# A decoder block's stick-breaking attention: scores by two products over all 128 rows, the weights' last product on GpSimd

## The chip, the cores and the metric

One core of one Trainium2 chip runs the whole kernel. The metric is the device time of one execution in microseconds (us).

## The reference

One decoder layer in float32: 1024 tokens of width 1024. It has eight heads of strictly causal stick-breaking attention and eight heads of latent attention (MLA) that share an input projection and an output projection, a gated feed-forward network with a short causal convolution, and a gated embedding at the end. What the change touches is the first of these:

```python
z = jnp.einsum('bqhd,bkhd->bhqk', q[:, start:end], k[:, :end]).astype(jnp.float32) * scale
strict = s_idx < t_idx
log_keep = jnp.where(strict, -jax.nn.softplus(z), 0.0)
log_keep_after = lax.cumsum(log_keep, axis=3, reverse=True) - log_keep
weights = jnp.where(strict, jnp.exp(jax.nn.log_sigmoid(z) + log_keep_after), 0.0)
outs.append(jnp.einsum('bhqk,bkhd->bqhd', weights.astype(v.dtype), v[:, :end]))
```

In words: the weight of key s for query t is sigmoid(z[t,s]) times the product of (1 - sigmoid(z[t,j])) over the keys j between s and t.

## The kernel before, in words

Every matrix product of the kernel is done in float32r with each operand split into a high part and a low part (`split`, lines 90 to 97: ScalarE copies the high part, VectorE or GpSimd subtracts it from the source to get the low one), and the small low-times-low term is dropped.

Stage 1 normalises and transposes the tokens. Stage 2, which the change touches, treats the eight stick-breaking heads as four pairs of two heads. A head has two units, g = 0 for the query blocks 0 to 3 (128 queries each) and g = 1 for the blocks 4 to 7. For block i, `sb_softmax` (lines 624 to 647) works on n = 128 (i + 1) keys, in one piece if n is at most 512 and otherwise in two halves (so a head has 12 pieces and 4608 columns of scores):

- TensorE forms the scores of a piece with two products: line 636, where the stationary operand holds the high part of the 64 query features beside the low part and the moving one holds the high part of the keys twice (128 rows), and line 637, high part of the queries times low part of the keys (64 rows); then the mask (line 447, through `masked`).
- ScalarE makes two sigmoids of it, of -z into `kc` (line 640) and of z into `w` (line 641).
- VectorE makes the running product of `kc` from the right with one scan (line 643), and multiplies `w` by it, shifted by one (line 645).

`kc` has two buffers that take turns. `weighted_sum` (lines 449 to 488) then transposes the blocks of `w` on TensorE (line 459), splits them (line 468) and multiplies by the values (lines 473, 474); line 479 adds the two halves into `o`, and line 674 stores a pair's `o` to the DRAM, a DMA in GpSimd's queue.

`run_units` (lines 490 to 510) writes the softmax of the next unit between the steps of the weighted sum of the unit before. Other work is spread between these steps by `Fill` (lines 151 to 191): during a pair, the projection of the next pair's queries, keys and values (`project`, lines 224 to 238; six times 24 products of 128 x 512), during the last pair `mla_prepare(True)`, the keys and values of the MLA heads with their stores in GpSimd's queue (lines 567, 575, 580). `mla_prepare(False)`, the MLA heads' queries, comes before the units in the program, and runs beside the first pair; GpSimd rotates its eight tiles of queries (`rotate`, lines 141 to 146) and stores them (line 610). A scheduler then fixes the order of instructions on each engine; an engine works its queue in this order. What it puts in front depends on a priority: the fill has 500 steps less than the rest (`LATER[0]`).

Of the kernel before, what the change touches and what calls it, by code (L numbers as in the profile page):

```python
# [21 lines left out]
NT = 8          # token tiles  # L22
NK = 8          # chunks of D_MODEL
H = 512         # tokens of a half
HD = 64
DFF = 2816
NCH = DFF // P  # 22
# [8 lines left out]
# how the work between the steps of the attention is spread: steps of it per step  # L36
# [5 lines left out]
# how far the scheduler is to put it behind the attention  # L42
LATER = (500, 0, 0, 2000)
# tiles normalised together in each half, and those scaled on the scalar engine
# [5 lines left out]
def tile_hybrid_block(ctx: ExitStack, tc: tile.TileContext, a: dict, out: bass.AP):  # L50
# [39 lines left out]
    def split(h, l, src, gain=None, on_pool=False):  # L90
        """src (times a gain of each partition) as the sum of two float32r parts."""
        if gain is None:
            act.copy(h, src)  # L93
            (pool if on_pool else dve).tensor_tensor(l, src, h, ALU.subtract)  # L94
        else:
            act.activation(h, src, AF.Copy, scale=gain)
            dve.scalar_tensor_tensor(l, src, gain, h, ALU.mult, ALU.subtract)
# [9 lines left out]
    def split_w(src, width=512, gain=None, on_pool=False, where=None):  # L107
        """A weight block of the DRAM, split."""
# [11 lines left out]
    def rstd_dve(small, ssq, count, n, tag, bufs=None):  # L120
        """(ssq / count + eps) ** -0.5 on one engine: Newton steps from a guess by exponent."""
# [16 lines left out]
    def rotate(eng, p_, x1, x2, cs, sn, shape):  # L138
        """The rotation of the pairs (x1, x2), in place."""
# [11 lines left out]
    class Fill:  # L151
        """Work traced in small steps between those of a stage. A generator gives True where it
        leaves none of the stage's buffers open."""
# [6 lines left out]
        def add(self, g, later=0):  # L160
            """later: how far behind the rest the scheduler is to put this work."""
            self.gens.append((g, later))
# [32 lines left out]
    now = {}                    # the current stage's makers of banks and of small tiles  # L195
# [17 lines left out]
    def sb_tiles(c):  # L213
        """Keys of two heads twice, their low parts, values; queries come later."""
        t4 = lambda tag: ata.tile([P, S], F32R, tag=tag, name=nm(tag), bufs=3)
        ka, kb = t4("ka"), t4("kb")
        kl = t4("ka" if c % 2 == 0 else "kb")
        vt = [ata.tile([P, NT, P], F32R, tag="v", name=nm("v"), bufs=3) for _ in range(2)]
        return {"k": (ka, kb), "kl": kl, "v": vt}
# [4 lines left out]
    def project(ci, consume, ths=(0, 1), ws=None):  # L224
        """128 columns of the input projection, transposed, for each half of the tokens."""
# [16 lines left out]
    def to_q(tiles):  # L242
        """Queries: the high part beside the low part."""
        def consume(th, ps):
            if th == 0:
                tiles["q"] = (tile4("qa", 2), tile4("qb", 2))
            sl = slice(th * H, th * H + H)
            for e in range(2):
                q = tiles["q"][e]
                split(q[hs[e], sl], q[hs[1 - e], sl], ps[hs[e], :])  # L250
        return consume

    def to_k(tiles):
        def consume(th, ps):
            sl = slice(th * H, th * H + H)
            for e in range(2):
                k = tiles["k"][e]
                split(k[hs[e], sl], tiles["kl"][hs[e], sl], ps[hs[e], :])
                act.copy(k[hs[1 - e], sl], k[hs[e], sl])
# [17 lines left out]
    with tc.tile_pool(name="pre", bufs=1) as pre, \  # L277
# [29 lines left out]
        # masks (rows are queries, columns keys)  # L307
# [7 lines left out]
        def normed(th):  # L315
            """A half of the tokens normalised, transposed and split."""
# [28 lines left out]
        # rotary tables  # L345
# [38 lines left out]
        def latents(th):  # L384
            """The latents of a half of the tokens, normalised, their keys' part rotated."""
# [14 lines left out]
            # the narrower part's sum doubled, so that one mean serves both  # L400
# [48 lines left out]
    def weighted_sum(u, p_, ptr, pav, rate):  # L449
        """The transposed product of a unit's weights with its values."""  # L450
# [30 lines left out]
        # the columns divided by their sums of weights: a row of each, the same in every partition  # L481
# [8 lines left out]
    def run_units(units, softmax, p_, ptr, pav, rates):  # L490
        """Softmax of each unit traced between the steps of the sum before it."""
# [52 lines left out]
    def mla_prepare(kv_only):  # L544
        """Latents to keys, values (kv_only) or queries of all MLA heads, kept in the DRAM."""
# [66 lines left out]

    for z in (project(0, to_q(pairs[0])), mla_prepare(False)):
# [10 lines left out]
    def sb_softmax(u):  # L624
        rows = hs[u["e"]]
        g, w = u["g"], u["w"]
        z = u["tiles"]
        q, k, kl = z["q"][u["e"]], z["k"][u["e"]], z["kl"]
        for i in range(4 * g, 4 * g + 4):
            n = (i + 1) * P  # L630
            qs = slice(i * P, i * P + P)
            kc = kcs[flip[0] % 2]
            flip[0] += 1
            for c0, c1 in pieces(n):
                sc = one_bank(py, "sc")[:, :c1 - c0]
                pe.matmul(sc, q[:, qs], k[:, c0:c1], start=True, stop=False)
                pe.matmul(sc, q[rows, qs], kl[rows, c0:c1], start=False, stop=c1 < n)
# [7 lines left out]
            dve.tensor_tensor(w[i], w[i], kc[:, S - n + 1:S + 1], ALU.mult)  # L645
# [5 lines left out]
    def sb_pre(u):  # L651
        c, g, e = u["c"], u["g"], u["e"]
        if e == 0 and g == 0:
            fill.drain()
            sb_pre.o = atb.tile([P, S], F32, tag="o", name=nm("o"), bufs=2)
            if c < 3:
                z = sb_tiles(c + 1)
                pairs.append(z)
                for ci, f_ in ((c + 1, to_q), (c + 5, to_k), (c + 9, to_v)):
# [25 lines left out]
    # --- MLA heads; between them the output projection of the stick-breaking heads, then of the  # L685
    # --- MLA heads' first half of the tokens, then the FFN of this half
# [11 lines left out]
    def group_ssq(src, sq, s, ps):  # L698
        """Sums of the squares over the features of (128, 4, 128) in token layout."""
# [642 lines left out]
```

## Time and profile before

| | |
|---|---|
| three runs | 1587.54, 1590.11 and 1591.46 us, median 1590.11 |
| the profiled execution | span 1588.5 us from the first to the last instruction |
| TensorE (PE) busy | 1507.7 us, 95% of the span |
| weight loads (PEld) busy | 1214.6 us, 76% |
| VectorE (DVE) busy | 1079.6 us, 68% |
| ScalarE (ACT) busy | 844.2 us, 53% |
| GpSimd (POOL) busy | 271.1 us, 17% |
| stick-breaking attention | from the first scores at 104.4 us to the first MLA scores at 417 us |

How to read it: "busy" is the time that an engine works on instructions; matmuls overlap, so their durations add up to more than the time in which they follow each other, and the spacing of their starts is the better measure. [...] Idle time is listed with what ended it: a tile of another engine, a DMA, or "issue", time in which an engine waited for nothing that the profile shows.

### The profile page before, as it was taken

The page shows a single profiled execution, that of the slowest core. Times are in us where ns is not written, and L with a number is a line of the kernel's source. Part 1 is how long each engine was busy: PE and PEld are TensorE (multiplying, and loading weights), DVE is VectorE, ACT ScalarE, POOL GpSimd, SP SyncE. Part 2 cuts the span into 40 slices and gives each one's busy share as a digit, 9 for nine tenths or more (in the row PEclk, how much of TensorE's full clock was granted, in tenths as well). Part 3 has the DMA queues.
Part 4 walks back from the last instruction along what each step waited for, and adds up shares of the span by engine and source line. Part 5 has one row for each costly group of instructions (what it writes and reads, how often), then busy time and mean ns, then how long its engine had stood idle before and what let it go on. Part 6 is the DMA issues. An engine that isn't in the chain of part 4 may idle for free. (4 is left out here: it accounts for less than half of the span.)

```text
span 1588.5 us, 20809 instructions
## 1 busy us (share of the span) xinstructions
PE 1507.7 (95%) x7032; PEld 1214.6 (76%) x7032; DVE 1079.6 (68%) x2021; ACT 844.2 (53%) x1649; POOL 271.1 (17%) x313
## 2 busy tenths in 40 slices
PE   4998999999899897999999999999999999999996
PEld 3976877766678786778888888888888888888875
DVE  4558667799767868866567954544986556544698
ACT  6345555677667756645544544444554444444542
POOL 7104300002133425242113100000000000000033
PEclk9998999999889999999999999999999999999998
DMA  6031210113345525134445532333443323333455
GB/s 197 22 100 40 86 48 27 41 52 126 111 134 148 157 70 186 61 99 146 148 125 169 177 119 90 97 95 96 141 134 94 98 94 94 93 93 94 132 176 169
DMA packets 109211, 173.78 MB, mean 109 GB/s; under 512 B 10912, under 2 KB 47680, under 8 KB 109104
## 3 DMA queue, kind: packets, MB, share of 16 engines
q1 hardware_dynamic: 100400, 142.71, 29.7%
q0 software_dynamic: 8704, 29.74, 5.0%
q8 instruction: 55, 0.90, 0.2%
q14 instruction: 52, 0.43, 0.1%
HBM read 142.26 MB, written 30.15 MB: 109 GB/s over the span
## 5 line engine op out<-in xcount | busy, mean ns | idle before, releaser
L93 ACT CAST wh<-ws 128x512 fp32r<-128x512 f32 x296 | 183.1, 620 | 213.3 <-PE mm L891 105.8
L94 DVE TENSOR_TENSOR wl<-ws,wh 128x512 fp32r<-128x512 f32 x281 | 199.9, 713 | 139.7 <-ACT wh L93 74.5
L889 PE MATMUL mm<-bh,wh 128*128 128x512 f32 x456 | 180.2, 395 | 0.0
L891 PE MATMUL mm<-bh,wh 128*128 128x512 f32 x456 | 180.1, 395 | 0.0
L94 DVE TENSOR_TENSOR fl<-f,fh 128x512 fp32r<-128x512 f32 x88 | 60.7, 691 | 118.0 <-PE mm L118 77.4
L94 DVE TENSOR_TENSOR tl<-tr,th 128x512 fp32r<-128x512 f32 x192 | 103.2, 549 | 33.9 <-ACT th L93 32.8
L895 PE MATMUL mm<-bh,wl 128*128 128x512 f32 x456 | 126.0, 396 | 0.0
L93 ACT CAST th<-tr 128x512 fp32r<-128x512 f32 x192 | 90.7, 483 | 64.6 <-PE tr L459 49.4
L643 DVE TENSOR_TENSOR_SCAN kc<-kc,one_f 128x128 f32<-128x128 f32 (+3 forms) x64 | 89.2, 1394 | 36.4 <-ACT kc L640 35.7
L93 ACT CAST fh<-f 128x512 fp32r<-128x512 f32 x88 | 54.6, 622 | 110.0 <-PE mm L117 84.3
L1160 POOL DMA_DIRECT2D x_dram<-fd x8 | 4.3, 538 | 615.1 <-DVE fd L1159 582.2
L459 PE MATMUL tr<-ident,w 128*128 128x128 f32 x576 | 103.3, 290 | 4.4 <-DVE tl L94 2.0
L889 PEld LDWEIGHTS mm<-bh,wh 128*128 128x128 f32 x456 | 85.9, 188 | 19.9
L891 PEld LDWEIGHTS mm<-bh,wh 128*128 128x128 f32 x456 | 85.9, 188 | 19.9
L895 PEld LDWEIGHTS mm<-bh,wl 128*128 128x128 f32 x456 | 85.6, 188 | 19.7
L116 PE MATMUL mm<-wh,fh 128*128 128x512 f32 x242 | 95.6, 396 | 0.0
L117 PE MATMUL mm<-wl,fh 128*128 128x512 f32 x242 | 95.3, 394 | 0.0
L459 PEld LDWEIGHTS tr<-ident,w 128*128 128x128 f32 x576 | 74.8, 148 | 20.0 <-DVE tl L94 3.7
L474 PE MATMUL av<-tl,v 128*128 128x512 f32 x192 | 75.8, 398 | 13.8 <-DVE tl L94 13.1
L473 PE MATMUL av<-th,v 128*128 128x512 f32 x192 | 79.2, 412 | 6.6 <-ACT th L93 3.6
L118 PE MATMUL mm<-wh,fl 128*128 128x512 f32 x242 | 82.5, 395 | 0.0
L640 ACT ACTIVATE kc<-sc 128x384 f32<-128x384 f32 (+4 forms) x96 | 47.7, 496 | 38.3 <-PE sc L447 22.9
(427 smaller groups left out, 3833.2 us busy)
## 6 DMA issues: line engine op xcount, KB each, us to landing
ws<-in_w_up SPq DMA_DIRECT2D x176, 256.0 KB, 2.6
ws<-in_w_down SPq DMA_DIRECT2D x88, 256.0 KB, 2.6
ws<-in_w_o SPq DMA_DIRECT2D x32, 256.0 KB, 2.8
xl<-x_dram SPq DMA_DIRECT2D x16, 512.0 KB, 3.9
ws<-in_w_in SPq DMA_DIRECT2D x24, 256.0 KB, 2.7
t<-o_dram SPq DMA_DIRECT2D x24, 256.0 KB, 3.2
xl<-o_dram SPq DMA_DIRECT2D x24, 256.0 KB, 2.8
xt<-in_x SPq DMA_DIRECT2D x8, 512.0 KB, 5.3
```

The lines of the kernel that those rows point to most:

```text
L93: act.copy(h, src)
L94: (pool if on_pool else dve).tensor_tensor(l, src, h, ALU.subtract)
L116: pe.matmul(ps, lh, rh, start=start, stop=False)
L117: pe.matmul(ps, lh, rl, start=False, stop=False)
L118: pe.matmul(ps, ll, rh, start=False, stop=stop)
L459: pe.transpose(tr[:, c:c + P], w[i][:, j * P:(j + 1) * P], ident)
L473: pe.matmul(av[:, lo:], v(j), th[:, lo:], start=j == 0, stop=False)
L474: pe.matmul(av[:, lo:], v(j), tl[:, lo:], start=False, stop=j == last)
L643: dve.tensor_tensor_scan(rev, rev, one_f[:, 0:1].to_broadcast([P, n]), 1.0, ALU.mult, ALU.mult)
L889: pe.matmul(ps, wh[:, k * P:(k + 1) * P], nh[:, kk], start=kk == 0, stop=False)
L891: pe.matmul(ps, wh[:, k * P:(k + 1) * P], nl[:, kk], start=False, stop=False)
L895: pe.matmul(ps, wl[:, k * P:(k + 1) * P], nh[:, kk], start=False, stop=kk == NK - 1)
```

## The change

Five edits, all in the stick-breaking part.

1. The keys lie as high part beside low part in one tile of 128 rows for each head (`to_k`), so their copy is gone. The queries lie twice (`to_q`): low part beside a copy of the high part (`q`), and high part beside zeros (`qz`, one of three tiles of 512 columns for each head of a pair, whose zero rows are written once). So line 642 of the new kernel multiplies `qz` by the keys (high times high, and zeros times low), and line 643 multiplies `q` by them (low times high and high times low): two products over 128 rows.
2. The product of `w` with the running product moves from VectorE (line 645) to GpSimd (line 651).
3. The projections of the next pair come in the order keys, values, queries instead of queries, keys, values.
4. `o` has one buffer instead of two.
5. The key tiles have two buffers instead of three.

```diff
     def sb_tiles(c):
...
-        t4 = lambda tag: ata.tile([P, S], F32R, tag=tag, name=nm(tag), bufs=3)
-        ka, kb = t4("ka"), t4("kb")
-        kl = t4("ka" if c % 2 == 0 else "kb")
+        ks = [ata.tile([P, S], F32R, tag=tag, name=nm(tag), bufs=2) for tag in ("ka", "kb")]
         vt = [ata.tile([P, NT, P], F32R, tag="v", name=nm("v"), bufs=3) for _ in range(2)]
-        return {"k": (ka, kb), "kl": kl, "v": vt}
+        return {"c": c, "k": ks, "v": vt}
...
             if th == 0:
                 tiles["q"] = (tile4("qa", 2), tile4("qb", 2))
+                tiles["qz"] = [[high_q[e][(2 * tiles["c"] + g) % 3] for g in range(2)]
+                               for e in range(2)]
             sl = slice(th * H, th * H + H)
             for e in range(2):
-                q = tiles["q"][e]
-                split(q[hs[e], sl], q[hs[1 - e], sl], ps[hs[e], :])
+                q, z = tiles["q"][e], tiles["qz"][e][th]
+                split(z[hs[e], :], q[hs[e], sl], ps[hs[e], :])
+                act.copy(q[hs[1 - e], sl], ps[hs[e], :])
...
                 k = tiles["k"][e]
-                split(k[hs[e], sl], tiles["kl"][hs[e], sl], ps[hs[e], :])
-                act.copy(k[hs[1 - e], sl], k[hs[e], sl])
+                split(k[hs[e], sl], k[hs[1 - e], sl], ps[hs[e], :])
...
+    high_q = [[atb.tile([P, H], F32R, name=f"qz{e}{i}") for i in range(3)] for e in range(2)]
+    for e in range(2):
+        for z in high_q[e]:
+            pool.memset(z[hs[1 - e], :].bitcast(F32), 0.0)
...
-                pe.matmul(sc, q[:, qs], k[:, c0:c1], start=True, stop=False)
-                pe.matmul(sc, q[rows, qs], kl[rows, c0:c1], start=False, stop=c1 < n)
+                pe.matmul(sc, qz[:, zs], k[:, c0:c1], start=True, stop=False)
+                pe.matmul(sc, q[:, qs], k[:, c0:c1], start=False, stop=c1 < n)
...
-            dve.tensor_tensor(w[i], w[i], kc[:, S - n + 1:S + 1], ALU.mult)
+            pool.tensor_tensor(w[i], w[i], kc[:, S - n + 1:S + 1], ALU.mult)
...
-            sb_pre.o = atb.tile([P, S], F32, tag="o", name=nm("o"), bufs=2)
+            sb_pre.o = atb.tile([P, S], F32, tag="o", name=nm("o"), bufs=1)
...
-                for ci, f_ in ((c + 1, to_q), (c + 5, to_k), (c + 9, to_v)):
+                for ci, f_ in ((c + 5, to_k), (c + 9, to_v), (c + 1, to_q)):
```

The scheduler makes a new order from this. Three places of it follow.

GpSimd's queue during the second head of the first pair. `w5` to `w7` are that head's weights, `qt` and `rt` belong to the rotation of the MLA queries, `q_dram` to their store. Before, the rotations of tiles stand there by themselves:

```order
L142 TENSOR_TENSOR rt_167_1092<-qt_163_1074,sin_t_85 128x128
L610 DMA q_dram_67<-qt_158_1048 128x4x192
L141 TENSOR_TENSOR rt_166_1091<-qt_163_1074,sin_t_85 128x128
L144 TENSOR_TENSOR qt_163_1074<-qt_163_1074,cos_t_84 128x8x16
L143 TENSOR_TENSOR qt_163_1074<-qt_163_1074,cos_t_84 128x8x16
L146 TENSOR_TENSOR qt_163_1074<-qt_163_1074,rt_166_1091 128x8x16
```

Now the products stand between them:

```order
L142 TENSOR_TENSOR rt_171_1129<-qt_167_1111,sin_t_85 128x128
L143 TENSOR_TENSOR qt_167_1111<-qt_167_1111,cos_t_84 128x8x16
L651 TENSOR_TENSOR w6_292_1688<-w6_292_1688,kc0_1267 128x896
L144 TENSOR_TENSOR qt_167_1111<-qt_167_1111,cos_t_84 128x8x16
L145 TENSOR_TENSOR qt_167_1111<-qt_167_1111,rt_171_1129 128x8x16
L651 TENSOR_TENSOR w7_293_1689<-w7_293_1689,kc1_1269 128x1024
L146 TENSOR_TENSOR qt_167_1111<-qt_167_1111,rt_170_1128 128x8x16
```

Of the 56 instructions of the eight rotations and their stores, 17 now stand between the first and the last product of this head, 2 ahead of them and 37 behind.

GpSimd's queue in the first head of the last pair. `k_dram`, `v_dram`, `kr_dram` and `o_dram` are stores, `kt` the first keys of the MLA heads. Before, there are only these:

```order
L989 TENSOR_TENSOR kt_835_3911<-ld_840_3916,kt_834_3910 96x512
L575 DMA k_dram_68<-lt_693_3379 128x512
L989 TENSOR_TENSOR kt_837_3913<-ld_841_3919,kt_836_3912 96x512
L580 DMA v_dram_70<-lt_695_3386 128x512
L567 DMA kr_dram_69<-lt_701_3412 32x512
L575 DMA k_dram_68<-lt_703_3419 128x512
```

Now the products of that head wait their turn between them:

```order
L995 TENSOR_TENSOR kt_831_3919<-ld_836_3924,kt_830_3918 96x512
L651 TENSOR_TENSOR w5_715_3484<-w5_715_3484,kc1_1269 128x768
L995 TENSOR_TENSOR kt_833_3921<-ld_837_3927,kt_832_3920 96x512
L577 DMA k_dram_68<-lt_689_3387 128x512
L582 DMA v_dram_70<-lt_691_3394 128x512
L680 DMA o_dram_63<-o_481_2536 128x1024
L569 DMA kr_dram_69<-lt_697_3420 32x512
L651 TENSOR_TENSOR w6_716_3485<-w6_716_3485,kc0_1267 128x896
L577 DMA k_dram_68<-lt_699_3427 128x512
L651 TENSOR_TENSOR w7_717_3486<-w7_717_3486,kc1_1269 128x1024
```

TensorE where the second pair begins. `pj` are projections, `sc` scores. Before, the pair's first scores stand behind 90 of the projections' products for that pair and are followed by the rest of them:

```order
L637 MATMUL sc_365_1971<-kb_201_1263,qa_231_1366 128x256
L447 MATMUL sc_365_1971<-mask_sb_78,ident_r_76 128x128
L116 MATMUL pj_278_1595<-hTh_2_96,wh_264_1510 128x512
L117 MATMUL pj_278_1595<-hTl_4_98,wh_264_1510 128x512
L118 MATMUL pj_278_1595<-hTh_2_96,wl_265_1511 128x512
```

Now all but four of the 144 (queries last) come first, and what follows the scores are the projections of the third pair (`pj_349`):

```order
L118 MATMUL pj_322_1813<-hTh_2_96,wh_306_1721 128x512
L643 MATMUL sc_353_1933<-ka_198_1272,qa_318_1790 128x128
L449 MATMUL sc_353_1933<-mask_sb_78,ident_r_76 128x128
L643 MATMUL sc_360_1978<-ka_198_1272,qa_318_1790 128x256
L449 MATMUL sc_360_1978<-mask_sb_78,ident_r_76 128x128
L116 MATMUL pj_349_1907<-hTh_1_95,wh_344_1897 128x512
```

So the first pair's four units and the MLA queries are done before the projections of the second pair begin, where these used to run beside the last of them.

## Rows read from the trace of the kernel before

**Rows 1.** By stretch: us; PE, PEld, DVE, ACT, POOL busy; clock; DMA; GB/s.
```profile
104.40:131.00 26.60, 24.61 (x102) 17.73 (x100) 21.07 (x26) 17.52 (x41) 0.00 (x0) 0.84 0.16 38
131.00:168.00 37.00, 33.51 (x154) 26.72 (x154) 30.87 (x31) 22.70 (x53) 28.00 (x45) 0.89 0.20 64
...
194.60:273.50 78.90, 78.90 (x362) 58.74 (x362) 55.65 (x74) 47.86 (x104) 0.55 (x1) 1.00 0.12 38
273.50:318.10 44.60, 44.60 (x208) 33.66 (x206) 33.53 (x46) 26.59 (x55) 0.56 (x1) 1.00 0.11 36
318.10:348.00 29.90, 28.80 (x144) 20.56 (x143) 26.51 (x38) 20.80 (x47) 0.00 (x0) 1.00 0.11 32
348.00:380.30 32.30, 30.09 (x146) 21.52 (x143) 30.08 (x42) 23.29 (x52) 12.75 (x21) 1.00 0.53 179
380.30:404.60 24.30, 20.00 (x81) 13.18 (x80) 23.37 (x32) 16.23 (x36) 0.00 (x0) 0.81 0.05 14
```

**Rows 2.** Waits, 104 to 404 us: who waited for what, us, times, longest.
```profile
PEld sc L637 <- issue: 22.0, 86, 0.5
...
PEld sc L447 <- issue: 10.1, 46, 0.4
```

**Rows 3.** Timeline of TensorE: a masked piece of scores, then an unmasked one.
```profile
239.75 0.39 PE L636 MATMUL sc<-kb,qb 128*128 128x512 f32 x1
240.06 0.49 PE L637 MATMUL sc<-kb,qb 64*128 64x512 f32 x1
240.48 0.33 PE L447 MATMUL sc<-mask_sb,ident_r 128*128 128x128 f32 x1
240.65 0.45 PE L118 MATMUL pj<-hTh,wl 128*128 128x512 f32 x1
240.94 0.40 PE L116 MATMUL pj<-hTh,wh 128*128 128x512 f32 x1
...
241.64 0.31 PE L636 MATMUL sc<-kb,qb 128*128 128x320 f32 x1
241.88 0.41 PE L637 MATMUL sc<-kb,qb 64*128 64x320 f32 x1
242.21 0.50 PE L116 MATMUL pj<-hTh,wh 128*128 128x512 f32 x1
242.55 0.39 PE L117 MATMUL pj<-hTl,wh 128*128 128x512 f32 x1
```

**Rows 4.** The same timeline: two projections that follow each other.
```profile
238.82 0.39 PE L117 MATMUL pj<-hTl,wh 128*128 128x512 f32 x1
239.05 0.39 PE L118 MATMUL pj<-hTh,wl 128*128 128x512 f32 x1
```

**Rows 5.** Timeline of TensorE: MLA scores of 96 rows beside a mask of 128.
```profile
417.82 0.22 PE L1066 MATMUL sc<-kt,ql 96*128 96x128 f32 x1
417.88 0.28 PE L447 MATMUL sc<-mask_ml,ident_r 128*128 128x128 f32 x1
417.99 0.34 PE L1066 MATMUL sc<-kt,ql 96*128 96x256 f32 x1
```

**Rows 6.** Stretches 104 to 403 us, line 643 alone, then line 645 alone.
```profile
sum 299.00, DVE 89.18; mean DVE 11.15
...
sum 299.00, DVE 51.53; mean DVE 6.44
```

**Rows 7.** Groups of GpSimd by line and shape: busy, mean ns, idle before.
```profile
L1271 POOL TENSOR_TENSOR ge<-ge,g_post_ple 128x512 f32<-128x512 f32 x15 | 20.2, 1356 | 40.7 <-ACT junk L1270 40.6
...
L989 POOL TENSOR_TENSOR kt<-ld,kt 64x1024 fp32r<-64x1024 f32 x5 | 12.1, 2427 | 7.2 <-ACT kt L987 6.0 <-issue 1.2
```

**Rows 8.** Timelines of VectorE and GpSimd: start, us, instruction.
```profile
157.37 3.42 DVE L643 TENSOR_TENSOR_SCAN kc<-kc,one_f 128x896 f32<-128x896 f32 x1 [1.09 <-ACT kc L640]
...
370.53 2.02 DVE L643 TENSOR_TENSOR_SCAN kc<-kc,one_f 128x896 f32<-128x896 f32 x1 [0.58 <-ACT kc L640]
...
152.05 1.93 POOL L144 TENSOR_TENSOR qt<-qt,cos_t 128x128 f32<-128x128 f32 x1
```

More of the change, by code (lines that the diff above doesn't have):

```diff
@@ L624, in sb_softmax @@
     def sb_softmax(u):
-        rows = hs[u["e"]]
         g, w = u["g"], u["w"]
         z = u["tiles"]
-        q, k, kl = z["q"][u["e"]], z["k"][u["e"]], z["kl"]
+        q, qz, k = z["q"][u["e"]], z["qz"][u["e"]][g], z["k"][u["e"]]
         for i in range(4 * g, 4 * g + 4):
@@ L631, in sb_softmax @@
             qs = slice(i * P, i * P + P)
+            zs = slice((i - 4 * g) * P, (i - 4 * g) * P + P)
             kc = kcs[flip[0] % 2]
```

## Prediction

> **What bounds the kernel now.** I first read the span by stretches, one for each of the eight heads (a head begins at its first scan; heads 3 and 4 share a row, and the time between heads 2 and 3 is left out) [rows 1]. The reader should compare PE with the length of the stretch. In heads 3 to 5 it is the whole stretch (78.9 of 78.9 us and 44.6 of 44.6, at full clock): there projections fill every gap and TensorE alone sets the pace. In heads 1, 2, 6, 7 and 8 it falls short by 1.1 to 4.3 us, and VectorE stands at 21.1 of 26.6, 30.9 of 37.0, 26.5 of 29.9, 30.1 of 32.3 and 23.4 of 24.3 us: there the chain scores, sigmoids, scan, product, transposes counts too, and VectorE is its longest link. GpSimd does almost nothing, but for the rotations in head 2 (28.0 us, 45 instructions) and stores and first keys in head 7 (12.75 us).
>
> Second, the waits: the two largest that TensorE's weight loads have with no releaser stand around the 64-row score product, ahead of line 637 (22.0 us over 86 times) and of the mask behind it (10.1 us over 46) [rows 2].
>
> Third, TensorE's timeline gives a piece's real price by the spacing of starts. A product of 512 columns is followed by the next after 0.23 us (238.82 to 239.05) [rows 4]. A masked piece takes from 239.75 to the second projection behind it at 240.94, which is 1.19 us [rows 3]. At the normal pace these four would take 0.23 + 0.23 + 0.11 (the mask, by the 0.11 behind the one in [rows 5]) + 0.23 = 0.80 us. The unmasked piece of 320 columns and one projection take 0.91 us (241.64 to 242.55), against 0.145 + 0.145 + 0.23 = 0.52. Both lose 0.39 us. What the two have in common is the product over 64 rows between others over 128.
>
> **The change, part by part.**
>
> *Two products over 128 rows.* The count and the columns of the matmuls stay; if the 0.39 us belongs to the 64 rows, it goes. Per head that is 12 pieces x 0.39 = 4.7 us, in all 96 x 0.39 = 37 us: the upper end. The lower end is nothing, if the loss comes from the score tiles themselves. I take the whole, because products of 96 rows beside a mask of 128 follow each other after 0.06 and 0.11 us, with no such loss [rows 5], so switching operands or groups alone does not make it. But it shortens the time only where TensorE sets the pace: in heads 3 to 5, 3 x 4.7 = **-14 us**. Elsewhere it is bounded by the chain, below.
>
> *The product on GpSimd.* VectorE loses 51.53 us, 6.4 a head, and keeps scans of 89.18 us, 11.1 a head [rows 6]. GpSimd's price for two f32 inputs comes from 1.356 us for 512 columns and 2.427 for 1024 (64 partitions) [rows 7]: 2.09 ns a column and 0.285 us an instruction. A head has 4608 columns in eight products, so 4608 x 2.09 ns + 8 x 0.285 = 11.9 us, and 96 us in all, nearly twice VectorE's. For heads 3 to 5 that is hidden: scan and product together need 11.1 + 11.9 = 23 us of heads of about 40 to 45.
>
> What is not free is the company. The scan of 896 columns took 3.42 us at 157.37, while GpSimd rotated, and 2.02 us at 370.53; beside VectorE a rotation's instruction of 128 x 128 took 1.93 us, against a mean of 28.0 / 45 = 0.62 [rows 8, 1]. So the two engines stretch each other; a scan lost 1.40 us once. How much of the 12 us a head is lost to VectorE lies between nothing and all of it.
>
> [...]
>
> Head by head, with both edits:
>
> - Head 1 (TensorE 24.6 of 26.6 us): between -4.7 (TensorE's gain whole) and 11.9 - 6.4 = +5.5 (the product in the chain, as much longer); I take the middle, **+0.5**.
> - Head 2 (33.5 of 37.0): GpSimd's 28.0 us of rotations and 11.9 of products no longer fit, and it works its queue in order. Only 17 rotation and store instructions stand between the products, so the head itself can be shorter by up to 4.7; I take **-3**, since scans and rotations meet here as in [rows 8]. The other 37 follow the last product: 37 x 0.62 = 23 us of tail. TensorE's last MLA-query products wait for buffers that come free with the fifth tile's store, some 16 instructions or 10 us into the tail; the head's last transposes and value products give it about 4 us meanwhile. So **+6** (0 if the rest of TensorE's work covers it, +10 if none does). The projections of pair 2, now behind this, cannot fill the gap.
> - Head 6 (28.8 of 29.9): TensorE falls to 24.1, VectorE to 26.5 - 6.4 = 20.1, GpSimd stands at 11.9. The bounds are -4.7 and 20.1 + 11.9 - 29.9 = +2.1, if VectorE and GpSimd only take turns. TensorE is the nearer limit: **-3**.
> - Head 7 (30.1 of 32.3): GpSimd has 12.75 + 11.9 = 24.7 us in one queue, and products stand behind stores that wait for ScalarE. Bounds -4.7 and 30.1 - 6.4 + 11.9 - 32.3 = +3.3; **-2**.
> - Head 8 (20.0 of 24.3, clock 0.81): there is no fill, so the chain sets it. Bounds 17.0 + 11.9 - 24.3 = +4.6, and -6.4 if VectorE alone was the limit; near the middle, **-0.5**. The very last product, of 1024 columns, is on the path with 2.43 us in place of about 1.43 (51.53 / 8 / 4608 x 1024): **+1**.
>
> *The rest.* The six zero fills lie before the first product, when GpSimd has nothing else: nothing; without that cover some 4 us (six by the 0.6 of a small GpSimd instruction). The copies on ScalarE move from keys to queries one for one; ScalarE is at most at 72% of a stretch (23.3 of 32.3 us in head 7): nothing. Queries last means that the first scores of a pair wait for all its projections; in pairs 2 to 4 the pair before covers that, as TensorE has its work in any case. One buffer of `o`: a pair's store now stands ahead of the next pair's first product in GpSimd's queue, and 140 projection products, 32 us, lie between; nothing. In the last pair that store is one of those of head 7. Two key buffers: a tile is written again two pairs later, when its readers are done; nothing.
>
> Sum: +0.5 - 3 + 6 - 14 - 3 - 2 - 0.5 + 1 = **-15 us**. I take one back for the different order of the MLA part, where nothing is meant to change: -14. The profiled execution spans 1588.5 us; the three runs' median is 1590.1, 1.6 above it. From the median: **1576 us**.
>
> **The rivals.**
>
> *TensorE gives back everything.* If fill is abundant enough that TensorE sets the pace in heads 1, 2, 6 and 7 too and the tail of rotations is covered, 25 to 37 us go: 1553 to 1565. For it: TensorE is at 90% or more of these four stretches. Against it: in heads 6 to 8 the fill is used up, and head 8 already runs at clock 0.81 for want of work.
>
> *The penalty stays.* If 0.39 us belongs to the piece (its score tile, its release by ScalarE) and not to the 64 rows, the -14 falls away, heads 6 and 7 gain perhaps 2 and the rest costs what it costs: +0.5 + 6 - 2 + 0.5 = +5, 1592 to 1600. For it: no row of this trace shows two 128-row score products. Against it: [rows 5], and that the issue idle stands just at lines 637 and 447 [rows 2].
>
> [...]
>
> *GpSimd's product blocks VectorE* (slower). If scan and product never run together and VectorE queues behind each product, a head's VectorE and GpSimd times add: head 6 +2.1, head 7 +3.3, head 8 +4.6, head 1 +0.5, head 2 +5 and its tail +8 (each stretched as in [rows 8]); against -14 in heads 3 to 5, which have the room. That is +9.5: about 1599.5, between 1593 and 1606. It decides once more than about half of the 12 us is lost to VectorE in each head, since below that TensorE's 24 us is still the longer. For it: 3.42 against 2.02 us. Against it: VectorE's operations on PSUM, and its idle time, can take the overlap.
>
> **How the numbers follow.** Chances: forecast 0.58 (1568 to 1587: its open terms are head 2's tail, 0 to +10, and heads 6 to 8, each by 2 or 3 us); all given back 0.16; blocked 0.16; penalty stays 0.10. The range leaves out most of the first rival's lower half and the blocked case's upper half: 1559 to 1598. A measurement can tell 0.3%, 4.8 us, from no change. Slower by more (over 1594.9): 0.14 of the blocked case and 0.06 of the last, 0.20. Within: 0.02 and 0.04, and 0.08 of the forecast's end at 1587: 0.14. Faster: 0.16 + 0.50 = 0.66.
>
> **What would show it.** Right: the second score product starts 0.23 us after the first on 512 columns and the issue idle ahead of it is gone; GpSimd's products sum to 96 us or somewhat more; VectorE loses 50 us in these stretches less what scans gain; heads 3 to 5 are each 4 to 5 us shorter; between the second head and the second pair, TensorE waits some us for MLA query tiles and GpSimd; the first MLA scores come near 403 us in place of 417. Wrong: score pieces as long as before; scans far above 89 us in all, or products far above 96; heads 6 to 8 longer than before; or a difference of more than a few us behind 417 us, for which none of these steps gives a reason.

## The result, and the profile after

The changed kernel takes 1580.83 us (median of 13 runs, 1575.81 to 1584.68) against 1590.11 (13 runs, 1584.09 to 1594.50): ratio 0.9941, 95% interval 0.9925 to 0.9957, which is 9.3 us faster. The forecast was 14 us faster.

Two rows of the changed kernel's profile (costliest groups) answer to [rows 6]:

```profile
L651 POOL TENSOR_TENSOR w<-w,kc 128x128 f32<-128x128 f32 (+3 forms) x64 | 83.0, 1301 | 157.9 <-DVE kc L649 84.8
L649 DVE TENSOR_TENSOR_SCAN kc<-kc,one_f 128x128 f32<-128x128 f32 (+3 forms) x64 | 101.0, 1587 | 21.6 <-ACT kc L646 21.4
```

The products take 83.0 us on GpSimd (51.5 on VectorE before), and the scans, whose code was not touched, went from 89.2 to 101.0 us.

TensorE's timeline of the changed kernel, a masked piece of 512 columns, answers to [rows 3]:

```profile
245.97 0.40 PE L642 MATMUL sc<-kb,qz 128*128 128x512 f32 x1
246.20 0.39 PE L643 MATMUL sc<-kb,qb 128*128 128x512 f32 x1
246.43 0.22 PE L449 MATMUL sc<-mask_sb,ident_r 128*128 128x128 f32 x1
246.49 0.45 PE L118 MATMUL pj<-hTh,wl 128*128 128x512 f32 x1
246.77 0.30 PE L642 MATMUL sc<-kb,qz 128*128 128x320 f32 x1
```

From 245.97 to the second instruction behind the mask at 246.77 it takes 0.80 us, where it was 1.19. In the list of waits the two "issue" rows of [rows 2] are gone; the largest waits between TensorE and the engines that feed it are others now (104 to 404 us; who waited for whom, us, times, longest):

```profile
POOL w L651 <- DVE kc L649: 84.8, 22, 29.0
ACT th L93 <- PE tr L461: 27.6, 33, 3.2
DVE tl L94 <- ACT th L93: 25.4, 28, 2.2
...
PEld av L476 <- DVE tl L94: 21.5, 24, 2.7
...
PE av L476 <- DVE tl L94: 15.1, 17, 2.5
```

The value products (line 476) wait for `tl`, the low part of the transposed weights, which VectorE makes. The same two rows stood before at 7.3 us (7 times) and 5.6 us (6 times). An engine's idle time may show in both rows, so they are not added.

How much of TensorE's gain became idle time? The stretch from the first scores to the first MLA scores is cut where the second pair's first scan starts. The columns are the stretch, its length, then busy time of PE, PEld, DVE, ACT, POOL, the clock granted to TensorE as a share of full speed, the DMA share and GB/s. Before:

```profile
104.40:194.60 90.20, 84.72 (x386) 66.17 (x384) 66.69 (x79) 52.24 (x116) 34.99 (x56) 0.91 0.22 67
194.60:416.90 222.30, 214.08 (x990) 155.98 (x989) 175.68 (x238) 140.42 (x306) 13.86 (x23) 0.97 0.16 52
```

After:

```profile
104.40:209.70 105.30, 93.77 (x469) 78.37 (x468) 60.36 (x73) 59.58 (x132) 54.04 (x73) 0.95 0.23 69
209.70:404.40 194.70, 175.71 (x917) 142.66 (x915) 147.01 (x181) 130.81 (x292) 76.46 (x70) 0.96 0.16 54
```

The second part again, cut between heads 3 to 5 and heads 6 to 8, before and after:

```profile
194.60:318.10 123.50, 123.50 (x568) 92.40 (x567) 89.19 (x119) 74.45 (x159) 1.11 (x2) 1.00 0.12 37
318.10:416.90 98.80, 90.58 (x424) 63.58 (x422) 86.49 (x121) 65.97 (x147) 12.75 (x21) 0.93 0.22 72
```

```profile
209.70:307.40 97.70, 94.02 (x495) 78.55 (x494) 69.65 (x86) 64.34 (x143) 31.70 (x25) 1.00 0.11 33
307.40:404.40 97.00, 81.69 (x423) 64.11 (x422) 77.36 (x97) 66.47 (x149) 44.76 (x46) 0.93 0.22 76
```

The first part grew because the queries, now last, bring more of the second pair's projections into it. That is counted from the groups by line, in the kernel before (104.4 to 194.6 us) and in the changed one (104.4 to 209.7):

```profile
L116 PE MATMUL pj<-hTh,wh 128*128 128x512 f32 x30 | 11.8, 394 | 0.0
```

```profile
L116 PE MATMUL pj<-hTh,wh 128*128 128x512 f32 x53 | 21.2, 400 | 0.0
```

Lines 117 and 118 show the same counts, so the first part has 3 x (53 - 30) = 69 of these products more. Some ten of them are the first pair's own: before, they stood ahead of 104.4 us, and in the changed kernel the first scores come 1.8 us later, at 106.2, with TensorE busy up to there. The other 59 left the second part (342 before, 283 now), and with them eight transposes of values, four value products and a mask. That is 59 x 0.23 = 13.6 us and an estimated 2 us for the rest, by the spacing of their starts: 15.6 us. With as much work in each part, the first, taken from its first scores, went from 105.8 to 103.5 us and the second from 206.7 to 194.7: -2.3 and -12.0, in all -14.3, of which the later start takes 1.8 back. TensorE's busy time fell by 8.3 us (there the granted clock rose too, 0.91 to 0.95) and by 22.8, and its idle time rose by 6.0 (5.5 to 11.5) and by 10.8 (8.2 to 19.0). So **TensorE got 31 us of the 37, and 17 of these came back as waiting.**

All the work that left the second part left heads 3 to 5: there 123.5 - 15.6 = 107.9 us became 97.7, and TensorE, which never stood idle there before, does so for 3.7 us. Heads 6 to 8 went from 98.8 to 97.0 us, and the idle time there from 8.2 to 15.3.

Behind the stage the profile after takes 3.1 us longer (first MLA scores to the end, 1174.7 against 1171.6), although that code is the same. One row in it grew by about as much: TensorE's wait of the value products for VectorE's split, from 417 us in the kernel before and from 405 us in the changed one:

```profile
PE av L474 <- DVE tl L94: 7.5, 8, 2.4
```

```profile
PE av L476 <- DVE tl L94: 11.9, 10, 3.0
```

The scheduler's order there differs a little between any two of these kernels. The kernel before, the changed one and eleven of the runs that follow have the same code behind the stage, and it takes 1166.5 to 1182.1 us in their profiles, one execution each. No run separated the 3.1 us from chance, and this part stays open.

### The profile page after: what moved, and what is told of

It is laid out like the page before. It is cut to its first block, busy times and chain, and to the rows that moved or that the text cites. A ratio compares the mean times of both kernels' runs of the same rounds, so it can differ in the third digit from the quotient of the medians.

```text
span 1579.1 us, 20935 instructions
## 1 busy us (share of the span) xinstructions
PE 1479.0 (94%) x7032; PEld 1214.0 (77%) x7032; DVE 1042.4 (66%) x1957; ACT 840.3 (53%) x1649; POOL 356.4 (23%) x383
## 5 line engine op out<-in xcount | busy, mean ns | idle before, releaser
L93 ACT CAST wh<-ws 128x512 fp32r<-128x512 f32 x296 | 182.8, 620 | 222.5 <-PE mm L897 107.9
L651 POOL TENSOR_TENSOR w<-w,kc 128x128 f32<-128x128 f32 (+3 forms) x64 | 83.0, 1301 | 157.9 <-DVE kc L649 84.8
L649 DVE TENSOR_TENSOR_SCAN kc<-kc,one_f 128x128 f32<-128x128 f32 (+3 forms) x64 | 101.0, 1587 | 21.6 <-ACT kc L646 21.4
```

Of the source, the lines that this page charges most:

```text
L649: dve.tensor_tensor_scan(rev, rev, one_f[:, 0:1].to_broadcast([P, n]), 1.0, ALU.mult, ALU.mult)
L651: pool.tensor_tensor(w[i], w[i], kc[:, S - n + 1:S + 1], ALU.mult)
```

## The experiments

Theory A: the score edit gives TensorE some 29 us; a product on GpSimd and a scan on VectorE exclude each other, which lengthens scans and delays splits and gives part of it back. Rival B: VectorE's relief carries the gain. Rival G: the exclusion is harmless, the mere length of the chain holds TensorE up. Rival C (E and H are later forms of it): the order of the projections costs time. Rival D, of e4: VectorE is the scarcer engine beside the rotations. Theory F, of e6: the move to GpSimd is worth its gain, but for the queue behind the rotations.

All ratios are against the kernel before, timed on the same chip beside the run.

| run | median us | ratio, 95% interval |
|---|---|---|
| the change | 1580.8 | 0.9941, 0.9925 to 0.9957 |
| e1: change, product on VectorE | 1577.9 | 0.9942, 0.9920 to 0.9964 |
| e2: before, product on GpSimd | 1584.9 | 0.9976, 0.9961 to 0.9992 |
| e3: change, queries first | 1571.4 | 0.9901, 0.9882 to 0.9921 |
| e4: change, MLA rotations on VectorE | 1577.5 | 0.9944, 0.9924 to 0.9963 |
| e5: change, half the queries first | 1578.4 | 0.9933, 0.9907 to 0.9959 |
| e6: e5 with the product on VectorE | 1584.4 | 0.9968, 0.9949 to 0.9986 |
| e8: before, queries last | 1591.5 | 1.0013, 0.9997 to 1.0028 |
| e9: change, ones in PSUM, two banks | 1576.0 | 0.9912, 0.9889 to 0.9935 |
| e10: change, ones in SBUF, two banks | 1586.8 | 0.9982, 0.9964 to 1.0000 |
| e11: e9, half the queries first | 1572.4 | 0.9898, 0.9868 to 0.9927 |
| e12: e10 with the product on VectorE | 1598.4 | 1.0059, 1.0039 to 1.0079 |

### The two large edits, one at a time (e1, e2)

```diff
-            pool.tensor_tensor(w[i], w[i], kc[:, S - n + 1:S + 1], ALU.mult)
+            dve.tensor_tensor(w[i], w[i], kc[:, S - n + 1:S + 1], ALU.mult)
```

> The changed kernel with the product of w and kc back on VectorE; everything else as changed. Theory A (the score edit brings TensorE 29 us and the product on GpSimd gives part of it back, because VectorE's scans grew from 89 to 101.5 us and the splits of the transposed weights come later): faster than the changed kernel, 1566 to 1576 us, scans back at 90 us, TensorE's wait of value products for the split tile (25 us summed over matmuls and weight loads less 5) down by half. Rival B (VectorE's relief of 51 us is what let heads 6 to 8 get shorter, the score edit brings only the 14 us of heads 3 to 5): slower than the changed kernel, 1583 to 1590 us.

For the second run the same line of the kernel before goes the other way.

> The kernel before with only its line 645 moved to GpSimd; scores as before with the 64-row product. Theory A: slower than the kernel before by 3 to 12 us, 1593 to 1602 us, scans at about 100 us, TensorE's issue idle ahead of the 64-row product unchanged at about 22 us. Rival B: faster than before by 3 to 8 us, 1582 to 1587 us.

On e1 both theories missed: without the move to GpSimd the change is worth the same (0.9942 against 0.9941), where A wanted a clear gain and B a clear loss. (e1 keeps the other four edits; of them only the order was also run by itself, in e8.) On e2 B was right and A wrong: the move alone, on the kernel before, gains 0.24% (3.8 us), although its scans do grow, as A said. The issue idle stays (waits of that run, 104 to 404 us, beside [rows 2]):

```profile
L643 DVE TENSOR_TENSOR_SCAN kc<-kc,one_f 128x128 f32<-128x128 f32 (+3 forms) x64 | 96.6, 1513 | 42.7 <-ACT kc L640 42.4
```

```profile
PEld sc L637 <- issue: 21.6, 82, 0.4
...
PEld sc L447 <- issue: 9.2, 43, 0.4
```

So the gains are -0.58% and -0.24% alone and -0.59% together: in the totals they don't add. In the stage itself they nearly do, by one profile of each: from the first scores to the first MLA scores it takes 312.5 us before, 302.3 in e1, 305.6 in e2 and 298.2 in the change. The part behind the stage, with the same code, takes 1166.5 us in e1's profile and 1174.7 in the change's, so by these profiles much of what makes their totals equal lies outside of what was edited.

A also expected the wait for `tl` to fall by half in e1. It didn't: e1 first, then e2.

```profile
PE av L476 <- DVE tl L94: 12.5, 19, 1.4
```

```profile
PE av L474 <- DVE tl L94: 5.1, 9, 1.4
```

In e1 no product on GpSimd meets a scan, and TensorE waits 12.5 us for `tl` (15.1 in the change). In e2 they do meet, beside the old scores, and it waits 5.1 (5.6 before). TensorE's idle time says the same (heads 3 to 5, then 6 to 8, in e1; heads 3 to 5 in e2):

```profile
204.62:309.31 104.69, 97.72 (x493) 80.74 (x492) 80.46 (x108) 63.75 (x142) 0.56 (x1) 0.97 0.10 33
309.31:406.64 97.33, 81.93 (x426) 63.94 (x424) 87.73 (x123) 67.65 (x151) 14.38 (x21) 0.93 0.22 73
```

```profile
193.63:315.16 121.53, 121.53 (x556) 90.21 (x554) 74.56 (x94) 72.25 (x156) 32.20 (x25) 1.00 0.10 33
```

Heads 3 to 5 have 7.0 us of idle time in e1 and none in e2, heads 6 to 8 have 15.4 in e1, and the whole stage has 32.9 there against 30.6 in the change. **So the waiting comes with the faster scores, whichever engine does the product.** Scans of 88.1 us in e1 against 101.0 say that VectorE is better off there in one respect, and carries 50 us of products in another. Which of two opposite effects of the move is how large needed a run that has one without the other.

### Scan and product by themselves (m1)

The program has no attention in it; between barriers it runs only the two operations, on 128 x 1024 in f32.

```diff
+    for _ in range(6):
+        scan(one_f)
+        product()
+    barrier()
+    for _ in range(12):
+        scan(one_p)
+        product()
```

> A program that leaves the whole block out and runs, between barriers: 6 scans of 128 x 1024 on VectorE alone, 6 products on GpSimd alone, 6 of both at once, 12 of both at once with the scan's second operand in PSUM, 24 low-part subtractions with one PSUM operand beside products, 6 products on VectorE. Theory A (scan and product exclude each other as a whole): alone 2.28 and 2.07 us; together each pair takes about 4.35 us; with the second operand in PSUM the scan stays at 2.3 us and the product at 2.1; the low-part subtraction keeps its 0.68 us. Rival (they only slow each other by shared bandwidth): together each pair takes 2.5 to 3.5 us, and the operand in PSUM changes little.

VectorE's timeline (start, us, instruction; equal neighbours are put into one row with their count):

```profile
3.46 13.92 DVE L84 TENSOR_TENSOR_SCAN kc<-kc,one_f 128x1024 f32<-128x1024 f32 x6 [0.35 <-ACT kc L96]
32.93 25.86 DVE L84 TENSOR_TENSOR_SCAN kc<-kc,one_f 128x1024 f32<-128x1024 f32 x6 [15.55 <-ACT kc L96]
59.42 27.82 DVE L84 TENSOR_TENSOR_SCAN kc<-kc,one_p 128x1024 f32<-128x1024 f32 x12 [0.63 <-ACT kc L96]
88.90 17.37 DVE L91 TENSOR_TENSOR kc<-src_p,kc 128x512 f32<-128x512 f32 x24 [1.66 <-ACT kc L96]
147.27 7.52 DVE L88 TENSOR_TENSOR w<-w,m 128x1024 f32<-128x1024 f32 x6 [41.01 <-ACT w L97]
```

GpSimd's:

```profile
18.04 14.42 POOL L88 TENSOR_TENSOR w<-w,m 128x1024 f32<-128x1024 f32 x6 [15.46 <-ACT w L97]
32.91 23.73 POOL L88 TENSOR_TENSOR w<-w,m 128x1024 f32<-128x1024 f32 x6 [0.46 <-ACT kc L96]
59.44 28.98 POOL L88 TENSOR_TENSOR w<-w,m 128x1024 f32<-128x1024 f32 x12 [2.79 <-ACT kc L96]
```

Alone, a scan takes 13.92 / 6 = 2.32 us and a product 14.42 / 6 = 2.40. Together, six of each need 25.86 us, 4.31 a pair: they go by turns, though not perfectly (4.72 would be the sum). With the column of ones in PSUM the scan takes 27.82 / 12 = 2.32 and the product 28.98 / 12 = 2.42 at the same time: no loss at all. The low-part subtraction, one operand in PSUM, takes 17.37 / 24 = 0.72 us beside products. The rival's 2.5 to 3.5 us a pair is out. The turns come although the scan's second operand in SBUF is one column that is read over and over, and where that column lies is, but for the number of pairs, all that differs between 4.31 us a pair and 2.42. What in the chip makes the two take turns, no run shows.

That it is turns and not an even slowing of both can be seen in the changed kernel. VectorE, then GpSimd, where the first head ends:

```profile
121.50 3.34 DVE L649 TENSOR_TENSOR_SCAN kc<-kc,one_f 128x896 f32<-128x896 f32 x1
...
125.54 3.35 DVE L649 TENSOR_TENSOR_SCAN kc<-kc,one_f 128x1024 f32<-128x1024 f32 x1
...
129.41 1.91 DVE L649 TENSOR_TENSOR_SCAN kc<-kc,one_f 128x128 f32<-128x128 f32 x1
```

```profile
121.41 1.55 POOL L651 TENSOR_TENSOR w<-w,kc 128x768 f32<-128x768 f32 x1 [2.17 <-DVE kc L649]
124.98 1.77 POOL L651 TENSOR_TENSOR w<-w,kc 128x896 f32<-128x896 f32 x1 [2.02 <-DVE kc L649]
129.04 2.00 POOL L651 TENSOR_TENSOR w<-w,kc 128x1024 f32<-128x1024 f32 x1 [2.29 <-DVE kc L649]
```

The product at 129.04 runs until 131.04. The scan of 128 columns that VectorE takes up at 129.41 ends at 131.32, 0.28 us later; unhindered it takes 0.42 (at 107.36 us in the kernel before). The product kept its usual time (2.00 us; the mean of its shape is 2.07).

### The exclusion taken away inside the kernel (e9, e10)

In both runs the tile with the column of ones in PSUM takes one of the projections' three banks, so they keep two; the runs differ only in what the scan reads.

```diff
-    x_cm, px = psum("px", 2)
+    x_cm, px = psum("px", 1)
+    one_p = px.tile([P, H], F32, tag="one", name="one_p")
+    dve.memset(one_p, 1.0)
...
-            dve.tensor_tensor_scan(rev, rev, one_f[:, 0:1].to_broadcast([P, n]), 1.0,
+            dve.tensor_tensor_scan(rev, rev, one_p[:, 0:1].to_broadcast([P, n]), 1.0,
```

(the last pair of lines in e9 alone)

> The changed kernel with the scan's second operand, the column of ones, in a PSUM bank that is taken from the projections (two banks for them in place of three). Theory A (the scans lose 12 us to GpSimd's products, which exclude a scan with two SBUF operands, and with them the splits of the transposed weights and TensorE's value products come late): scans total 88 to 91 us in place of 101.5, products 80 to 82 us, and 3 to 8 us faster than the control with the same two banks and the ones in SBUF. Rival G (the time lost to the exclusion lies beside TensorE's work or other waits; what holds TensorE up is the length of the chain scores, sigmoids, scan, product, transposes, splits itself): scans as in theory A, but within 2.5 us of the control.

> The control: as the run with the ones in PSUM, with two banks for the projections, but the scan reads the ones from SBUF as in the changed kernel. Both theories: scans at 100 to 103 us; the bank that is missing costs 0 to 6 us against the changed kernel (1579 to 1587 us).

With the ones in PSUM, 104 to 412 us:

```profile
L651 DVE TENSOR_TENSOR_SCAN kc<-kc,one_p 128x128 f32<-128x128 f32 (+3 forms) x64 | 85.8, 1347 | 25.3 <-ACT kc L648 24.9
```

The control:

```profile
L651 DVE TENSOR_TENSOR_SCAN kc<-kc,one_f 128x256 f32<-128x256 f32 (+7 forms) x63 | 101.9, 1624 | 19.4 <-ACT kc L648 19.0
```

The scans lose 16 us (one of the 64 is missing from the control's trace), products go from 81.8 to 77.9, and the whole is **10.8 us faster**, 1576.0 against 1586.8, with intervals that do not touch. TensorE's wait for `tl` falls (the control, then with the ones in PSUM, 104 to 404 us):

```profile
PE av L476 <- DVE tl L94: 14.6, 18, 1.7
```

```profile
PE av L476 <- DVE tl L94: 9.5, 16, 1.6
```

The first MLA scores come at 402.2 in place of 410.5. So with two banks the exclusion costs more than the 3 to 8 us expected, and it is not harmless, as rival G held. The other half of G, that the chain itself holds TensorE up, is not refuted: without the exclusion TensorE still stands idle for 33.5 of the stage's 299.4 us (40.3 of 310.0 in the control). The bank itself cost 6 us by medians (1580.8 to 1586.8). How much the exclusion costs with three banks was not tried.

### What the move is worth without its cost (e12)

> The control with two banks and the ones in SBUF, with the product of w and kc on VectorE instead of GpSimd. Theory A (what the move to GpSimd takes off VectorE, 51 us, is largely given back by the exclusion: a product of 83 us that keeps scans from running, 12 us of longer scans and later splits): within 4 us of the control, 1583 to 1590 us. Rival B (VectorE's relief is worth more than the exclusion costs): 5 us or more slower than the control, 1591 us or above.

The control with the line moved back to VectorE is 12 us slower (1.0059 against 0.9982; differences of ratios times 1590). Here B is right and A's "within 4 us" is wrong. The move was thus measured on four kernels: -12 us (e12 to e10), -5.6 (e6 to e5; these two intervals overlap), -3.8 (before to e2) and nothing (e1 to the change, 0.9942 to 0.9941). In the stage itself, by one profile each, it brought 7.8, 1.5, 6.9 and 4.1 us. With two banks both sides are known: the move without exclusion goes from 1.0059 to 0.9912, 23 us, and the exclusion gives 11 of these back. Why the move is worth nothing in the total just in the change as it stands, these runs don't settle: each of them also has an order of its own from the scheduler, ahead of the stage and behind it too.

### The order of the projections (e3, e5, e6, e8, e11)

```diff
-                for ci, f_ in ((c + 5, to_k), (c + 9, to_v), (c + 1, to_q)):
+                for ci, f_ in ((c + 1, to_q), (c + 5, to_k), (c + 9, to_v)):
```

> The changed kernel with the projections of the next pair in the old order, queries, keys, values. Theory A holds the order to be worth little, since TensorE's work is the same: within 4 us of the changed kernel (1577 to 1585 us). Rival C (queries last keep the first pair's scores from overlapping the second pair's projections, and cost the 6 us that the prediction put on head 2's tail): 1573 to 1577 us, and the second pair's first scan more than 5 us earlier than at 209.7 us.

In this kernel the queries of the next pair's second half are written into a zero-padded tile that the second head has yet to read, so part of that head's scores are formed from the wrong queries; the amount of work is the same. Its ratio is 0.9901, 6 us less than the change's, and the second pair's first scan began at 173.9. But the tiles that force the order are part of what is to be explained, so a second run kept the data right:

```diff
-                for ci, f_ in ((c + 5, to_k), (c + 9, to_v), (c + 1, to_q)):
-                    fill.add(project(ci, f_(z)), LATER[0])
+                fq = to_q(z)
+                fill.add(project(c + 1, fq, ths=(0,)), LATER[0])
+                for ci, f_ in ((c + 5, to_k), (c + 9, to_v)):
+                    fill.add(project(ci, f_(z)), LATER[0])
+                fill.add(project(c + 1, fq, ths=(1,)), LATER[0])
```

> The changed kernel with the next pair's projections in the order queries of the first 512 tokens, keys, values, queries of the last 512 tokens (the weights of the queries are split twice). The three tiles with zeros suffice for this. Theory E (the order of the projections cost some 6 to 9 us, since the first pair's scores, scans and products and the MLA queries run without the overlap with the second pair's): 1570 to 1575 us, second pair's first scan at 175 to 195 us in place of 209.7. Rival (what the queries-first run saved came from reading tiles that were already overwritten, so without their waits): within 3 us of the changed kernel, 1578 to 1584 us.

> The kernel of the run with the first half's queries first, with the product of w and kc on VectorE. Theory F (the product on GpSimd is worth the 3.8 us it gave alone, and was worth nothing in the changed kernel only because of its queue behind the MLA rotations in head 2): 3 to 6 us slower than that kernel, 1574 to 1580 us. Rival G (with 128-row scores the product on GpSimd brings nothing anywhere, as VectorE's scans get 12 us longer and the splits come later): within 2 us of it.

> The kernel before with only the order of the projections changed to keys, values, queries. Theory E (the order costs the same by itself, because the stretch between the second head and the second pair can't be filled): 4 to 9 us slower than before, 1592 to 1598 us. Rival H (the order costs only where GpSimd has products between the rotations): within 2.5 us of before.

> The kernel with the scan's ones in PSUM (two banks for the projections), and the next pair's projections in the order first-half queries, keys, values, second-half queries. Theory A with E (exclusion and order are two separate losses): 1568 to 1574 us, 2 to 8 us faster than with the ones in PSUM alone. Rival G (once the chain of a head is what holds TensorE up, an earlier first score of a pair only moves the idle time): within 2.5 us of the kernel with the ones in PSUM, 1574 to 1579 us.

In e5 the second pair's first scan starts at 186.5 us, 23 before the change's, and yet the first MLA scores come at 406.6 (404.4 in the change) and the total can't be told from it. An earlier start of a pair alone bought nothing here: TensorE's idle time in the stage is 33.5 us, against 30.6. e6 is 5.6 us slower than e5, as F said (3 to 6 us), where G wanted 2 at most; F's reason was not tried by itself. On the kernel before, the order by itself costs 2 us within its error (1.0013, 0.9997 to 1.0028), so E's 4 to 9 us is out. Whether e3's 6 us come from the order proper or from work that need not wait for those tiles stays open; e5 splits the queries' weights twice and is no exact undoing. With the ones in PSUM the order of e5 brings 2 us by the ratios (0.9912 to 0.9898), and the intervals overlap. **At 1572.4 us and 0.9898, e11 beats both kernels**; its interval (0.9868 to 0.9927) and the change's (0.9925 to 0.9957) just meet.

### The rotations off GpSimd (e4)

```diff
-                rotate(pool, atb, qt[:, :, 64:80], qt[:, :, 80:96], cs, sn, [8, 16])
+                rotate(dve, atb, qt[:, :, 64:80], qt[:, :, 80:96], cs, sn, [8, 16])
```

> The changed kernel with the rotations of the MLA queries on VectorE in place of GpSimd (56 instructions, of which 8 are stores that stay on GpSimd's queue). Theory A (GpSimd's instructions hold VectorE up wherever they meet; the rotations sit between the first products): heads 1 and 2 no longer than now, the tail of 37 instructions gone, 0 to 5 us faster than the changed kernel. Rival D (VectorE is the scarcer engine there, 41 of 54 us busy in heads 1 and 2, and 48 more instructions of about 0.3 us put 14 us on it): 2 to 8 us slower.

The total is the change's (0.9944), so there is no sign of rival D's loss of 2 to 8 us, nor of a gain. The second pair starts 6 us sooner (203.7 us), 4.3 of which are there at the first scores already (101.9 against 106.2), with 8 of the 159 projection products, 1.8 us, not yet done, and the stage ends 6.4 us sooner in its profile, at 398.0; the part behind the stage took 1182.1 us against 1174.7 there, so the total shows nothing of it.

## Why the prediction was right, and where its terms were off

**Right:** the direction, the range (1559 to 1598) and the cause. The 0.39 us a piece belonged to the 64-row product: a masked piece takes 0.80 us as worked out, the issue idle is gone, e1 has the gain without the move, and e2, which keeps that product, keeps the idle. Whether its rows or its operands make that product dear, no run tried. Nor do the rivals' ends hold: TensorE did not give all back (31 us of busy time, 9 of the total), and the penalty did not stay.

**Luck:** by the profiles, whose spans differ by 9.4 us, heads 1 and 2 came out at -2.3 us, heads 3 to 5 at -10.2, heads 6 to 8 at -1.8, the start ahead of the first scores at +1.8 and the part behind the stage at +3.1. The prediction had +3.5, -14, -4.5, 0 and +1. The first pair's miss of 5.8 us hides more than half of the 10.4 us that the other terms were short, and that the total came within 5 us of the forecast is luck to that extent.

**The first pair** was put at +0.5 - 3 + 6 = +3.5 us. TensorE's idle time did grow by 6.0 there, but not where the prediction put it: behind the last product, from 158 to 210 us, TensorE's listed waits are 0.8, 0.7, 0.6 and 0.2, about 2 us. The step "TensorE's last MLA-query products wait for buffers that come free with the fifth tile's store" was sized three times too large; TensorE hardly waits beside GpSimd's tail.

**Heads 3 to 5** were put at -14 us, because "there projections fill every gap and TensorE alone sets the pace". That held for the kernel before, and the step that failed is to let it hold for the faster one too. TensorE's busy time fell by 13.9 us, as worked out, and 3.7 came back as idle time. "For heads 3 to 5 that is hidden" held, by contrast: with the product on VectorE (e1) the idle time there is 7.0 us. **Heads 6 to 8**, put at -4.5, gave TensorE 8.9 us, and 7.1 came back. That scan and product get in each other's way is not the main reason: TensorE stands idle in the stage for 30.6 us in the change, 32.9 in e1, where they never meet, and 33.5 in e9, where they don't exclude each other (with two banks). What the list of waits names is the end of the chain of scan, product, transposes and splits, which the faster TensorE reaches too soon (`av` for `tl`, 15.1 us in PE's row against 5.6 before, 12.5 in e1 and 9.5 in e9).

**The start**, the "nothing" of the zero fills among it: the first scores come 1.8 us later. e1 has the same fills and its first scores at 104.3, and over these kernels they come between 100.5 and 106.6 us, so this is no cost of the fills.

**The product on GpSimd** was taken at 96 us and took 83.0; the price was built on [rows 7], one of whose rows has half the partitions. **The scans'** loss, left between nothing and all of the products' time, was 12 us in the change and 16 between e10 and e9.

**The blocked rival** had scan and product never run together, and m1 shows nearly that (4.31 us a pair, 2.32 and 2.40 alone); it put the loss too high: it would have needed half of the 12 us a head, and VectorE lost 12 / 8 = 1.5. In the rows above GpSimd starts a product right when a scan ends, and VectorE then has splits with a PSUM operand to do, which m1 shows running beside products (0.72 us each); that this is why so little is lost was argued, not tried. And **the relief of VectorE**, which the prediction costed at nothing in the saturated heads, is worth more than that: 23 us of the total, with two banks and where nothing excludes it.

Behind the stage a loss of 1 us was taken and 3.1 were seen, with no step to explain it.

## What to carry to other kernels

Read a matmul's price from the spacing of starts: here a masked piece with a product over half the rows between full ones took 1.19 us, and 0.80 with a full product with zeros in it. Before moving an elementwise product from VectorE to GpSimd, look at the operands of what stays: here a scan with two of them in SBUF went by turns with the product on GpSimd (4.31 us a pair), and with one of them in PSUM, even a constant column, the two ran side by side (2.32 and 2.42 us). And when the bounding engine is relieved, price the chain behind it by what is late next, not by whether the busy times still fit.

## What was not expected

- With the second operand one column of ones in SBUF, read with stride zero, a scan waited until a GpSimd instruction ended, or nearly so (1.91 us for 128 columns in place of 0.42); moved to PSUM, the column was worth 10.8 us of 1587 in the kernel with two banks for the projections.
- The same product of 1024 columns takes 2.40 us on GpSimd in the small program and 2.07 in the kernel (mean of 8; groups by shape); why is open. On VectorE it takes 7.52 / 6 = 1.25 us.
- Taking one of three PSUM banks from the projections cost 6 us with the product on GpSimd (0.9941 to 0.9982), and some 19 with it on VectorE (e1 to e12, 0.9942 to 1.0059).
